# A two-layer streaming encoder step on one core: small attention and GLA products issued as closed clusters of one array shape

## The chip, the core and the metric

The kernel runs on one core of a Trainium2 chip. The metric is the device time of one execution in microseconds (us); before the change it is 2438.22 us, the median of three runs (2436.23 to 2441.65).

TensorE (PE) multiplies a stationary operand, which a weight load brings into its array of 128 by 128, with a moving operand, and writes to PSUM, which has eight banks of 128 partitions. A product whose stationary operand has fewer than 128 rows or columns uses a part of the array. The profile writes that shape as rows*columns (64*128). VectorE (DVE), ScalarE (ACT) and GpSimd (POOL) read the PSUM results and prepare operands. SyncE (SP) issues the DMAs.

## The reference, cut to what matters

Two layers; 2048 prompt tokens and 8 samples of 16 tokens, which are handled as 17 tiles of 128 tokens (the last one is the samples).

```
u = rms_norm(h) @ w_in                       # 1024 -> q, k, v, gate a, q b, k b, v b, gate b, forget gate
A = softmax(q k^T / 8, with a sink) v        # 8 heads of 64, 2 k/v heads, window of 128, in chunks of 64
B = gated linear attention (GLA), 4 heads, keys 64, values 128:
    S[t] = exp(g[t]) * S[t-1] + k[t] v[t]^T,   o[t] = q[t] S[t]
h = h + [A * silu(ga) ; rms_norm(B) * silu(gb)] @ w_out
h = h + sigmoid(rms_norm(h) @ w_pg) * (p @ w_pe)
```

For a prompt tile GLA is computed from products of 128 tokens: scores of the tile's own tokens with one another (masked; exponents are taken relative to a position near the pair, so the scores come from several scaled copies of queries and keys), scores times values, queries times the state S from the tiles before, and the update of S. Each of the eight samples has a state of its own, and for attention a cache of 128 older keys and values.

## The kernel before

The token tiles form five groups (0-2, 3-6, 7-10, 11-13, 14-16; the samples are tile 16). For each of two layers and five groups `phase_in` runs the projections and both attentions, then `phase_out` runs w_out, w_pg and w_pe. All weights are streamed from memory in pieces of 256 KB, which SP fetches and ACT (line 154) and DVE (line 84) split in a high and a low part. A big product is done in three passes, high by high, high by low, low by high (`mm3`, lines 322 to 324), each with a full 128*128 stationary operand and 256 to 512 moving columns.

Everything small is in plain fp32, whose products show as two records each. For a prompt tile, in the function and with the lines that the profile names:

- `attn_prompt`: scores L526, four products for each of two head pairs, 64*128, into two banks of the tag "s"; `softmax` (the exponentials are L487); the transposes L537, L538, L540 of the probabilities P; ACT and DVE copies to `ptf` and `pth`; outputs L560 (128*64) and L569 (64*64), eight products into two banks of the tag "o"; then `gate_mix` on DVE.
- `gla_exps` and `gla_scores`: E holds six scaled copies of queries and keys. Scores come from L733 (64*128), L738 (64*32) and L742 (64*64), 16 products in two banks "s"; a masked copy on DVE; L756 transposes the keys for the state update.
- `gla_prompt`: at·v L795 (128*128), E·S L798 (64*128), both into two banks "o"; the state update L802 (128*64).
- `gla_norm_gate` squares the output on ACT (L765), scales on POOL (L766, L768) and multiplies on DVE (L771); `gla_out` transposes it (L782) and writes the operand `mix` of w_out on ACT (L784) and DVE (L785).

For the sample tile `attn_sample` alternates a product with the cache (L623) and one with the new values (L624). `gla_sample` goes sample by sample: it loads a state by DMA, multiplies it with the queries (L834, transposed result), updates it (L840), and at the end copies the transposed results (line 856) and adds them to the output by products with the identity (L860), between the products L859.

The attention and GLA of each tile are Python generators that are put in a background queue, up to two at a time; `pump` advances them between the big products of the projections behind which they are to lie. This fixes priorities only. The scheduler orders each engine's instructions by priority and by when operands become ready, so a small cluster can be cut by big products or by another generator's rows.

PSUM before: two banks "mm" for big products, two "s", two "t", two "o". Where attention does not run, big products rotate through "mm", "s" and "o" (`pw`).

## Time and profile before

| what | value |
|---|---|
| median of three runs | 2438.22 us |
| span of the profiled execution, first to last instruction | 2437.0 us |
| instructions | 44522 |
| POOL's share, and that of the DMA queue of the weights | 28%, 36.7% of 16 engines |
| big products, passes of 256 columns into "mm" (six groups of 544 records) | about 157 us busy each |
| mean granted TensorE clock | 0.992 |

The profile is one execution taken apart by engine. A group of instructions is a line of the program, an engine, an operation and its tiles; "busy" is its time, the mean is that of one instruction. Since matmuls are pipelined, a mean is longer than the distance from one start to the next, so what a product costs in the stream is read from starts in the timeline. "xN" is the number of records. Releasers (after "<-") say what ended a wait.

### The profile page before, as it was taken

The numbers are of one execution on the slowest core, as the hardware profiler recorded it, in microseconds if no ns is written. First come the engines' busy times: TensorE is split into PE (matmuls) and PEld (weight loads), VectorE is DVE, ScalarE is ACT, GpSimd is POOL, SyncE is SP. The second block draws the span as 40 slices with busy tenths as digits, with TensorE's granted clock in tenths as the row PEclk, the third lists the DMA queues.
The fourth block names the chain that finished last, engine by engine and source line by source line (L and its number), as shares of the span: only waits on it lengthen the run. The fifth ranks groups of instructions, "written<-read, shape, count | busy, mean of one in ns | idle before, by whom it ended". The sixth has DMA issues, their size and how long they took to land.

```text
span 2437.0 us, 44522 instructions
## 1 busy us (share of the span) xinstructions
PE 2402.9 (99%) x16188; PEld 2151.0 (88%) x16188; DVE 1661.0 (68%) x3957; ACT 1304.1 (54%) x3087; POOL 691.0 (28%) x833
## 2 busy tenths in 40 slices
PE   8999999999999999999999999999999999999999
PEld 8899888897888989988998998888988889899889
DVE  7767765777567867764876687567775588577645
ACT  6556644555445655643665566445554456466434
POOL 4224212341214312422332152123312143133222
PEclk9999999999999999999999999999999999999999
DMA  5245222432144325523532442134321543355233
GB/s 161 87 137 153 83 70 92 139 116 80 36 150 147 103 79 176 160 85 108 170 114 87 158 144 85 55 116 137 105 71 35 168 144 101 100 163 153 86 103 123
DMA packets 160443, 279.15 MB, mean 115 GB/s; under 512 B 17840, under 2 KB 43824, under 8 KB 160224
## 3 DMA queue, kind: packets, MB, share of 16 engines
q1 hardware_dynamic: 159536, 275.43, 36.7%
q8 instruction: 127, 2.08, 0.4%
q10 hardware_dynamic: 688, 0.88, 0.1%
q14 instruction: 92, 0.75, 0.1%
HBM read 255.41 MB, written 20.71 MB: 113 GB/s over the span
## 4 chain that ended last, share of the span: by engine, by line
PE 90%; DVE 4%; DMA 2%; ACT 2%; issue 2%; POOL 0%; SPq 0%; DVEq 0%; POOLq 0%; ACTq 0%
PE pw L324 13%; PE pw L322 13%; PE pw L323 13%; PE mm L322 11%; PE mm L323 11%; PE mm L324 11%; PE s L526 3%; DVE w L84 2%; PE o L560 1%; PE s L733 1%; PE o L795 1%; DMA raw<-in_w_pe_dram 1%; PE o L798 1%; PE o L569 1%; PE t L802 1%
## 5 line engine op out<-in xcount | busy, mean ns | idle before, releaser
L84 DVE TENSOR_TENSOR w<-raw,w 128x512 fp32r<-128x512 f32 (+1 forms) x800 | 565.9, 748 | 60.3 <-ACT w L154 58.2
L154 ACT ACTIVATE w<-raw 128x512 fp32r<-128x512 f32 (+1 forms) x800 | 452.0, 625 | 138.6 <-DMA raw<-in_w_pe_dram 34.1
L324 PE MATMUL pw<-mix,w 128*128 128x384 f32 (+1 forms) x640 | 228.2, 360 | 0.0
L322 PE MATMUL pw<-mix,w 128*128 128x384 f32 (+1 forms) x640 | 226.6, 362 | 1.6 <-ACT mix L784 1.6
L323 PE MATMUL pw<-mix,w 128*128 128x384 f32 (+1 forms) x640 | 228.0, 358 | 0.0
L84 POOL TENSOR_TENSOR ot<-gth,hst 128x384 f32<-128x384 f32 (+1 forms) x79 | 103.1, 1306 | 249.3 <-DVE gth L1017 208.0
L487 ACT ACTIVATE P<-s,nm 128x192 f32<-128x192 f32 (+3 forms) x272 | 108.7, 413 | 108.8 <-DVE den L480 90.6
L322 PE MATMUL mm<-w,A 128*128 128x256 f32 x544 | 159.9, 294 | 0.0
L322 PE MATMUL mm<-w,B 128*128 128x256 f32 x544 | 159.9, 294 | 0.0
L323 PE MATMUL mm<-w,B 128*128 128x256 f32 x544 | 157.2, 289 | 0.0
L323 PE MATMUL mm<-w,A 128*128 128x256 f32 x544 | 156.9, 288 | 0.0
L324 PE MATMUL mm<-w,B 128*128 128x256 f32 x544 | 156.2, 287 | 0.0
L324 PE MATMUL mm<-w,A 128*128 128x256 f32 x544 | 156.1, 287 | 0.0
L84 POOL TENSOR_TENSOR acc<-sq,acc 128x384 f32<-128x384 f32 (+1 forms) x60 | 75.3, 1254 | 252.3 <-ACT sq L253 251.8
L84 POOL TENSOR_TENSOR E<-E,qkb 128x128 f32<-128x128 f32 (+1 forms) x160 | 105.0, 687 | 122.2 <-DVE qkb L670 48.7
L322 PEld LDWEIGHTS pw<-mix,w 128*128 128x128 f32 x640 | 120.4, 189 | 13.5 <-ACT mix L784 2.0
L324 PEld LDWEIGHTS pw<-mix,w 128*128 128x128 f32 x640 | 120.7, 189 | 10.9 <-issue 0.6
L84 POOL TENSOR_TENSOR xacc<-sq,xacc 128x384 f32<-128x384 f32 (+1 forms) x66 | 98.2, 1488 | 111.4 <-ACT sq L253 109.4
L323 PEld LDWEIGHTS pw<-mix,w 128*128 128x128 f32 x640 | 120.7, 189 | 10.0
L84 POOL TENSOR_TENSOR mix<-ga_t,mix 128x512 fp32r<-128x512 f32 x34 | 43.8, 1287 | 288.1 <-ACT mix L507 288.1
L322 PE MATMUL mm<-B,w 128*128 128x384 f32 (+1 forms) x320 | 117.8, 368 | 1.9 <-DVE yq L377 1.9
L322 PE MATMUL mm<-A,w 128*128 128x384 f32 (+1 forms) x320 | 117.3, 366 | 0.7 <-DVE yq L377 0.7
(279 smaller groups left out, 7327.4 us busy)
## 6 DMA issues: line engine op xcount, KB each, us to landing
raw<-in_w_in_dram SPq DMA_DIRECT2D x400, 256.0 KB, 3.3
raw<-in_w_out_dram SPq DMA_DIRECT2D x160, 256.0 KB, 3.3
raw<-in_w_pg_dram SPq DMA_DIRECT2D x160, 256.0 KB, 3.8
raw<-in_w_in_dram SPq DMA_DIRECT2D x40, 272.0 KB, 3.3
raw<-in_w_pe_dram SPq DMA_DIRECT2D x40, 256.0 KB, 3.6
hl<-in_h_dram SPq DMA_DIRECT2D x24, 192.0 KB, 3.5
hbuf<-ot SPq DMA_DIRECT2D x24, 192.0 KB, 2.8
hx<-hbuf SPq DMA_DIRECT2D x24, 192.0 KB, 4.0
```

What stands on the lines that cost most here:

```text
L84: (eng or G).tensor_tensor(out=out, in0=in0, in1=in1, op=op1)
L154: A.activation(out=w[:, 0, k0:k0 + 2, :], in_=r, func=ACTF.Copy)
L322: PE.matmul(out=out, lhsT=sh, rhs=mh, start=(i == 0), stop=False)
L323: PE.matmul(out=out, lhsT=sh, rhs=ml, start=False, stop=False)
L324: lastmm[0] = PE.matmul(out=out, lhsT=sl, rhs=mh, start=False, stop=(i == last)).ins
L487: A.activation(out=P[:, e, p0:p0 + wd], in_=ps[:, c, :wd], func=ACTF.Exp, scale=0.125, bias=nm[:, e:e + 1], accum_out=den[:, 0, e:e + 1])
L526: PE.matmul(out=lst[g][:, c, :wd], lhsT=qT[gs, ti, c * 256 + hp * 128:c * 256 + hp * 128 + 128], rhs=kk[gs, k0:k0 + wd], start=True, stop= ...
L560: PE.matmul(out=ot[c][gs], lhsT=vT[:, fs, gs], rhs=ptf[:, c, g], start=True, stop=not half)
L569: PE.matmul(out=ot[c][gs], lhsT=vT[hr, hf, gs], rhs=pth[hr, g], start=not full, stop=True)
L733: PE.matmul(out=pa[e][:, hp, :], lhsT=E[hs, 1, hp, :], rhs=E[hs, 0, hp, :], start=True, stop=True)
L795: PE.matmul(out=po[h % 2][:, hp, :], lhsT=at[:, h, :], rhs=vt[:, h * 128:h * 128 + 128], start=True, stop=False)
L798: PE.matmul(out=po[h % 2][:, hp, :], lhsT=E[hs, 5, hp, :], rhs=S[hs, hp, :], start=False, stop=True)
```

## The change

The products of a cluster are issued through a new function `chain`: the first one carries, as additional dependences, the last operands that the later ones need, and each later one is ordered behind its predecessor at high priority, so that nothing comes between. The two-bank tiles "s" and "o" replace pairs of one-bank tiles, and are held in a pool of their own (`banks_as("p")`) while attention runs; otherwise the four banks are single tiles for big products (`banks_as("w")`), and `pw` takes every third tile from "mm".

In `softmax` and in the masked copy of the GLA scores one instruction covers both banks where there were two. The GLA scores are cut in pieces of 64 rows by 32 columns (32 products in place of 16 for a prompt tile; the quarter that L733 computed only for L742 to overwrite is left out). In `gla_prompt` the four products of each kind follow one another. In `attn_sample` the 16 products with the cache come first, then the 16 with the new values. In `gla_sample` the states come in by two DMAs; the queries are spread over a masked copy `Em` (POOL), and queries times state go straight into the output accumulation, without the transposed intermediate, its copy and the identity products. Comments and doc strings are removed, which moves lines: `mm3` is L343 to L345, the attention transposes are L556, L557, L559, the key transposes L789, the output transposes L815.

```diff
-    ps_s = ctx.enter_context(tc.tile_pool(name="ps_s", bufs=2, space=bass.MemoryType.PSUM))
     ps_t = ctx.enter_context(tc.tile_pool(name="ps_t", bufs=2, space=bass.MemoryType.PSUM))
-    ps_o = ctx.enter_context(tc.tile_pool(name="ps_o", bufs=2, space=bass.MemoryType.PSUM))
+    banks = dict(pool=None, stack=None, n=0)
+
+    def banks_as(kind):
+
+        if banks["stack"] is not None:
+            banks["stack"].close()
+            banks["stack"] = None
+        if kind is None:
+            return
+        banks["n"] += 1
+        banks["stack"] = ExitStack()
+        banks["pool"] = banks["stack"].enter_context(
+            tc.tile_pool(name=f"ps_{kind}{banks['n']}", bufs=1, space=bass.MemoryType.PSUM, reuse_waits="tile"))
...
-        """any bank, where attention does not run"""
         rot[0] += 1
-        p, tg = ((ps_m, "mm"), (ps_s, "s"), (ps_m, "mm"), (ps_o, "o"), (ps_s, "s"), (ps_o, "o"))[rot[0] % 6]
-        return p.tile([128, n], F32, tag=tg, name="pw")
-
-    def po2(shape):
-        return [ps_o.tile(shape, F32, tag="o", name="o") for _ in range(2)]
-
-    def ps2(shape):
-        return [ps_s.tile(shape, F32, tag="s", name="s") for _ in range(2)]
+        if rot[0] % 3 == 1:
+            return pm(n)
+        return banks["pool"].tile([128, 512], F32, tag="w", name="pw", bufs=4)[:, :n]
+    def pair(tag):
+        return banks["pool"].tile([128, 2, 512], F32, tag=tag, name=tag, bufs=1)
+    def chain(prev, after=(), **kw):
+        if prev[0] is None:
+            prev[0] = PE.matmul(**kw).ins
+            for x in after:
+                tc.add_manual_dep(prev[0], x.name, mybir.DependencyInfo(mybir.DependencyClass.Sync, mybir.DependencyReason.DATA),
+                                  reason="operands of the products behind it")
+        else:
+            with tc.issue_after(prev[0]), tc.high_priority():
+                prev[0] = PE.matmul(**kw).ins
 
...
-                lst = [ps_s.tile([128, 2, 192], F32, tag="s", name="s") for g in range(2)]
+                lst = pair("s")[:, :, :384].rearrange("p g (c k) -> p g c k", c=2)
+                pv = [None]
...
-                        PE.matmul(out=lst[g][:, c, :wd], lhsT=qT[gs, ti, c * 256 + hp * 128:c * 256 + hp * 128 + 128],
-                                  rhs=kk[gs, k0:k0 + wd], start=True, stop=True)
+                        chain(pv, out=lst[:, g, c, :wd], lhsT=qT[gs, ti, c * 256 + hp * 128:c * 256 + hp * 128 + 128],
+                              rhs=kk[gs, k0:k0 + wd], start=True, stop=True)
...
-            ot = po2([128, 256])
+            ot = pair("o")[:, :, :256]
+            pv = [None]
...
-                        PE.matmul(out=ot[c][gs], lhsT=vT[:, fs, gs], rhs=ptf[:, c, g], start=True, stop=not half)
+                        chain(pv, (pr_, pq_), out=ot[gs, c], lhsT=vT[:, ti + c, gs], rhs=ptf[:, c, g], start=True, stop=not half)
...
+            ot = pair("o")[:, :, :256]
+            pv = [None]
+            for b in range(8):
+                for g in range(2):
+                    gs = slice(g * 64, g * 64 + 64)
+                    bc = slice((b % 4) * 64, (b % 4) * 64 + 64)
+                    chain(pv, out=ot[gs, b // 4, bc], lhsT=cv[:, b, gs], rhs=pts[g][0][:, b * 64:b * 64 + 64],
+                          start=b % 4 == 0, stop=False, skip_group_check=True)
+            for b in range(8):
+                for g in range(2):
+                    gs = slice(g * 64, g * 64 + 64)
+                    bc = slice((b % 4) * 64, (b % 4) * 64 + 64)
+                    chain(pv, out=ot[gs, b // 4, bc], lhsT=vo[b // 4][:, b % 4, gs], rhs=pts[g][1][:, b * 64:b * 64 + 64],
+                          start=False, stop=True, skip_group_check=True)
...
+                Em = ip.tile([128, 2, 2, 128], F32, name="Em")
+                G.memset(Em, 0.0)
...
+                for par in range(2):
+                    G.tensor_copy(Em[:, par].rearrange("p h (c two i) -> p two h c i", two=2, i=16)[:, par],
+                                  E[:, 0].rearrange("p h (c two i) -> p two h c i", two=2, i=16)[:, par])
...
-            ptt(E[:, 3, :, 64:128], E[:, 3, :, 64:128], qv[:, :, 64:128], ALU.mult)
+            done["e3"] = G.tensor_tensor(out=E[:, 3, :, 64:128], in0=E[:, 3, :, 64:128], in1=qv[:, :, 64:128], op=ALU.mult).ins
...
-            pa = ps2([128, 2, 128])
+            if sample:
+                E = E[0]
+            pa = pair("s")[:, :, :256].rearrange("p e (h t) -> p e h t", h=2)
             both = [slice(0, 64), slice(64, 128)]
+            pv = [None]
             for hp in range(2):
-                for e, hs in enumerate(both):
-                    PE.matmul(out=pa[e][:, hp, :], lhsT=E[hs, 1, hp, :], rhs=E[hs, 0, hp, :], start=True, stop=True)
+                for i in range(4):
+                    q = slice(32 * i, 32 * i + 32)
+                    k = slice(0, 64 if i < 2 and not sample else 128)
+                    for e, hs in enumerate(both):
+                        chain(pv, (done["e3"],), out=pa[q, e, hp, k], lhsT=E[hs, 1, hp, q], rhs=E[hs, 0, hp, k], start=True, stop=True)
                 if sample:
                     continue
                 for i in range(2):
                     for e, hs in enumerate(both):
-                        PE.matmul(out=pa[e][64 * i:64 * i + 32, hp, 64 * i + 32:64 * i + 64],
-                                  lhsT=E[hs, 2, hp, 64 * i:64 * i + 32], rhs=E[hs, 2, hp, 64 * i + 32:64 * i + 64],
-                                  start=True, stop=True)
-                for e, hs in enumerate(both):
-                    PE.matmul(out=pa[e][0:64, hp, 64:128], lhsT=E[hs, 3, hp, 0:64], rhs=E[hs, 3, hp, 64:128],
+                        chain(pv, out=pa[64 * i:64 * i + 32, e, hp, 64 * i + 32:64 * i + 64],
+                              lhsT=E[hs, 2, hp, 64 * i:64 * i + 32], rhs=E[hs, 2, hp, 64 * i + 32:64 * i + 64],
+                              start=True, stop=True)
+                for i in range(2):
+                    q = slice(32 * i, 32 * i + 32)
+                    for e, hs in enumerate(both):
+                        chain(pv, out=pa[q, e, hp, 64:128], lhsT=E[hs, 3, hp, q], rhs=E[hs, 3, hp, 64:128],
                               start=True, stop=True)
...
-            po = po2([128, 2, 128])
-            for hp in range(2):
-                for h in (2 * hp, 2 * hp + 1):
-                    PE.matmul(out=po[h % 2][:, hp, :], lhsT=at[:, h, :], rhs=vt[:, h * 128:h * 128 + 128], start=True, stop=False)
-                for h in (2 * hp, 2 * hp + 1):
-                    hs = slice((h % 2) * 64, (h % 2) * 64 + 64)
-                    PE.matmul(out=po[h % 2][:, hp, :], lhsT=E[hs, 5, hp, :], rhs=S[hs, hp, :], start=False, stop=True)
+            po = pair("o")[:, :, :256].rearrange("p e (h t) -> p e h t", h=2)
+            pv = [None]
+            for h in range(4):
+                chain(pv, deps, out=po[:, h % 2, h // 2, :], lhsT=at[:, h, :], rhs=vt[:, h * 128:h * 128 + 128], start=h < 2, stop=False,
+                      skip_group_check=True)
+            for h in range(4):
+                hs = slice((h % 2) * 64, (h % 2) * 64 + 64)
+                chain(pv, out=po[:, h % 2, h // 2, :], lhsT=E[hs, 5, h // 2, :], rhs=S[hs, h // 2, :], start=False, stop=True,
+                      skip_group_check=True)
             pu = pt([128, 2, 128])
             for h in range(4):
                 hp, hs = h // 2, slice((h % 2) * 64, (h % 2) * 64 + 64)
-                PE.matmul(out=pu[hs, hp, :], lhsT=ke[:, h * 64:h * 64 + 64], rhs=vt[:, h * 128:h * 128 + 128],
-                          start=True, stop=True)
+                chain(pv, out=pu[hs, hp, :], lhsT=ke[:, h * 64:h * 64 + 64], rhs=vt[:, h * 128:h * 128 + 128],
+                      start=True, stop=True)
...
+            st8 = []
+            for c in range(2):
+                x = ip.tile([128, 4, 2, 128], F32, tag="ptf", name="s0", bufs=2)
+                SP.dma_start(out=x, in_=a["s0"][l, 4 * c:4 * c + 4].rearrange("b p h v -> p b h v"))
+                st8 += [x[:, b] for b in range(4)]
+            yield
+            pv = [None]
+            for c in range(4):
+                pu = pt([128, 2, 2, 128])
+                for b in range(2):
+                    km = ip.tile([128, 256], F32, tag="qy", name="km", bufs=4)
+                    G.tensor_scalar(out=km, in0=ke, scalar1=cst[:, C_OH + 2 * c + b:C_OH + 2 * c + b + 1], scalar2=None, op0=ALU.mult)
+                    for h in range(4):
+                        hp, hs = h // 2, slice((h % 2) * 64, (h % 2) * 64 + 64)
+                        chain(pv, out=pu[hs, b, hp, :], lhsT=km[:, h * 64:h * 64 + 64], rhs=vt[:, h * 128:h * 128 + 128],
+                              start=True, stop=True)
...
+                yield
+            while sgb[ti] is None:
+                yield
+            po = pair("o")[:, :, :256].rearrange("p e (h t) -> p e h t", h=2)
+            for h in range(4):
+                chain(pv, out=po[:, h % 2, h // 2, :], lhsT=at[:, h, :], rhs=vt[:, h * 128:h * 128 + 128], start=h < 2, stop=False,
+                      skip_group_check=True)
             for b in range(8):
+                tb = slice(b // 2 * 32, b // 2 * 32 + 32)
                 for h in range(4):
+                    hs = slice((h % 2) * 64, (h % 2) * 64 + 64)
+                    chain(pv, out=po[tb, h % 2, h // 2, :], lhsT=Em[hs, b % 2, h // 2, tb], rhs=st8[b][hs, h // 2, :],
+                          start=False, stop=b % 2 == 1, skip_group_check=True)
```

What this does to the order on PE, at three places of layer 0. In each row stand the line, the operation, output and inputs, the output's size, and how many alike follow one another.

First, the GLA output of one prompt tile and the GLA scores of the next, in the second group (`at` the masked scores, `vb` the values, `S` the state, `ke` the scaled keys, `E` scaled queries and keys). PE before:

```order
L795 MATMUL o<-vb,at_89 128x128 x2
L798 MATMUL o<-S,E 128x128 x2
L795 MATMUL o<-vb,at_89 128x128 x2
L798 MATMUL o<-S,E 128x128 x2
L802 MATMUL t<-vb,ke 64x128 x4
L733 MATMUL s<-E 128x128 x2
L738 MATMUL s<-E 32x32 x4
L742 MATMUL s<-E 64x64 x2
L733 MATMUL s<-E 128x128 x2
L738 MATMUL s<-E 32x32 x4
L742 MATMUL s<-E 64x64 x2
L756 MATMUL t<-cst,E 128x128 x2
```

PE of the changed kernel at the same place (L116 is the first product of a chain, L122 the later ones):

```order
L116 MATMUL o<-vb,at_83 128x128
L122 MATMUL o<-vb,at_83 128x128 x3
L122 MATMUL o<-S,E 128x128 x4
L122 MATMUL t<-vb,ke 64x128 x4
L116 MATMUL s<-E 32x64
L122 MATMUL s<-E 32x64 x3
L122 MATMUL s<-E 32x128 x4
L122 MATMUL s<-E 32x32 x4
L122 MATMUL s<-E 32x64 x8
L122 MATMUL s<-E 32x128 x4
L122 MATMUL s<-E 32x32 x4
L122 MATMUL s<-E 32x64 x4
```

The output's three kinds now stand once each, and the scores, all of one stationary shape, have no change of it within the cluster.

Second, attention in the second group (`kT`, `qs` keys and queries, `P` probabilities, `ptf`, `pth` their transposes, `vT` values). PE before:

```order
L526 MATMUL s<-kT,qs 128x192 x2
L560 MATMUL o<-ptf,vT 64x256 x4
L569 MATMUL o<-pth,vT 64x256 x3
L537 MATMUL t<-cst,P 128x128
L569 MATMUL o<-pth,vT 64x256
L538 MATMUL t<-cst,P 128x128
L540 MATMUL t<-cst,P 128x128
L537 MATMUL t<-cst,P 128x128
L538 MATMUL t<-cst,P 128x128
L540 MATMUL t<-cst,P 128x128
L526 MATMUL s<-kT,qs 128x192 x2
```

PE of the changed kernel, the nearest clusters of the same group:

```order
L116 MATMUL s<-kT,qs 128x192
L122 MATMUL s<-kT,qs 128x192 x3
L556 MATMUL t<-cst,P 128x128
L557 MATMUL t<-cst,P 128x128
L559 MATMUL t<-cst,P 128x128
L556 MATMUL t<-cst,P 128x128
L557 MATMUL t<-cst,P 128x128
L559 MATMUL t<-cst,P 128x128
L345 MATMUL mm<-w,B_2334 128x256
```

The four score products stand together, where each half of two stood by itself before, with outputs and transposes of another tile between.

Third, the end of the group with the samples (`km`, `ats` the sample's masked keys and scores, `s_...` its states, `on` the normed output, `mix_...` operands of w_out). PE before:

```order
L802 MATMUL t<-vb,ke 64x128 x4
L834 MATMUL s<-Es,s_12942 128x16 x4
L322 MATMUL pw<-mix_11168,w 128x384
L323 MATMUL pw<-mix_11168,w 128x384
L324 MATMUL pw<-mix_11168,w 128x384
L840 MATMUL t<-vb,km 64x128 x4
L859 MATMUL o<-vb,ats 128x128 x2
L860 MATMUL o<-cst,ga_t 128x128
L859 MATMUL o<-vb,ats 128x128
L860 MATMUL o<-cst,ga_t 128x128
```

PE of the changed kernel:

```order
L345 MATMUL mm<-mix_11307,w 128x384
L122 MATMUL t<-vb,km 64x128 x8
L122 MATMUL t<-vb,ke 64x128 x4
L122 MATMUL o<-vb,ats 128x128 x4
L122 MATMUL o<-s_12891,Em 32x128 x16
L122 MATMUL o<-s_12893,Em 32x128 x16
L815 MATMUL t<-cst,on 128x128 x8
L343 MATMUL pw<-mix_11307,w 128x384
```

The update, the output and the state products follow one another without big products between them, and the transposes of the normed output of two tiles (`on`, x8) come directly behind.

More of the change, by code (lines that the diff above doesn't have):

```diff
@@ L479, in softmax @@
[L479 to L488 removed]
+            mv = mx.rearrange("p (i c) -> p i c", c=2)
@@ L489, in softmax @@
+            for e in range(4):
+                wd = ps.shape[3] if wd_of is None else wd_of[e % 2]
+                p0 = 0 if wd_of is None else 128 - 64 * (e % 2)
+                A.activation(out=P[:, e, p0:p0 + wd], in_=ps[:, e // 2, e % 2, :wd], func=ACTF.Exp, scale=0.125,
+                             bias=nm[:, e:e + 1], accum_out=den[:, 0, e:e + 1])
             A.activation(out=den[:, 1], in_=den[:, 1], func=ACTF.Exp)
@@ L568, in attn_prompt @@
                     if half:
-                        PE.matmul(out=ot[c][gs], lhsT=vT[hr, hf, gs], rhs=pth[hr, g], start=not full, stop=True)
+                        chain(pv, out=ot[gs, c], lhsT=vT[hr, ti + 1 - c, gs], rhs=pth[hr, g], start=not full, stop=True)
             gate_mix(ot, ti, 2)
@@ L751, in gla_scores @@
             av = at.rearrange("p (hp e) t -> p e hp t", e=2)
-            for e in range(2):
-                V.copy_predicated(av[:, e], m.unsqueeze(1).to_broadcast([128, 2, 128]), pa[e])
+            V.copy_predicated(av, m.unsqueeze(1).unsqueeze(1).to_broadcast([128, 2, 2, 128]), pa)
             pk = pt([128, 256])
@@ L1075, in hybrid_step @@
     S = None
+    banks_as("w")
     for i, (l, gi) in enumerate(seq):
```

133 lines of the change are left out of this document (44 added, 89 removed).

## The prediction, as it was made before the changed kernel had run

> **What bounds the kernel now.** I read the page's busy times first, then the chain of work that ended last, then the waits of PE.
>
> ```profile
> PE 2402.9 (99%) x16188; PEld 2151.0 (88%) x16188; DVE 1661.0 (68%) x3957; ACT 1304.1 (54%) x3087; POOL 691.0 (28%) x833
> PE 90%; DVE 4%; DMA 2%; ACT 2%; issue 2%; POOL 0%; SPq 0%; DVEq 0%; POOLq 0%; ACTq 0%
> PE pw L403 <- ACT w L154: 7.2, 1, 7.2
> PE pw L322 <- ACT gth L1014: 5.4, 2, 2.7
> PE mm L322 <- DVE yq L377: 2.7, 2, 1.9
> ```
>
> TensorE is busy 99% of the span and makes up 90% of the chain. The longest single wait of PE (7.2 us) is for weights. In the whole list of waits one small product of attention or GLA stands: L834, with 2.7 us (its row is below). The operands of the others are ready when PE comes to them. So a microsecond taken out of PE's own stream is a microsecond of the span, as long as no operand becomes late. The question is what the small products cost in that stream, and that is read from the timeline of PE: start, duration, and how many records a group has (one fp32 product is two records).
>
> ```profile
> 390.69 0.60 PE L795 MATMUL o<-vb,at 128*128 128x128 f32 x4
> 391.23 0.49 PE L798 MATMUL o<-S,E 64*128 64x128 f32 x4
> 391.65 0.71 PE L795 MATMUL o<-vb,at 128*128 128x128 f32 x4
> 392.29 0.49 PE L798 MATMUL o<-S,E 64*128 64x128 f32 x4
> 392.71 0.66 PE L802 MATMUL t<-vb,ke 128*64 128x128 f32 x8
> 393.30 0.49 PE L733 MATMUL s<-E 64*128 64x128 f32 x4
> 393.72 0.27 PE L738 MATMUL s<-E 64*32 64x32 f32 x8
> 393.92 0.33 PE L742 MATMUL s<-E 64*64 64x64 f32 x4
> 394.18 0.49 PE L733 MATMUL s<-E 64*128 64x128 f32 x4
> 394.60 0.27 PE L738 MATMUL s<-E 64*32 64x32 f32 x8
> 394.79 0.33 PE L742 MATMUL s<-E 64*64 64x64 f32 x4
> 395.06 0.44 PE L756 MATMUL t<-cst,E 128*128 128x128 f32 x2
> ...
> 395.45 0.28 PE L323 MATMUL mm<-w,B 128*128 128x256 f32 x1
> 395.57 0.28 PE L324 MATMUL mm<-w,B 128*128 128x256 f32 x1
> L795 PE MATMUL o<-vb,at 128*128 128x128 f32 x256 | 43.5, 289 | 0.0
> L738 PE MATMUL s<-E 64*32 64x32 f32 x512 | 17.7, 203 | 0.0
> ```
>
> This is the GLA output of one prompt tile (2.61 us, 390.69 to 393.30) and the GLA scores of the next (1.76 us, 393.30 to 395.06). The stationary shapes (128*128, 64*128, 128*64, 64*32, 64*64) change at each row. Two readings:
>
> - **The rate inside a shape.** Four records of L795 take 0.60 us where one takes 0.289 on average: (0.60 - 0.289) / 3 = 0.104 us a record, 0.81 ns a column.
> - **The price of a change of shape.** L733 has two products on two row halves, so two records of 128 columns one after the other: 2 x 0.104 = 0.21 of the 0.42 us until the next group starts; 0.21 is left over. L742: 0.26 - 2 x 64 x 0.81 ns = 0.16. L738: 0.20 - 2 x 32 x 0.81 ns = 0.15. I take 0.18 us a change.
>
> L738 also shows that pieces lying in different parts of the array run together: eight records end 0.27 us after the first began, and one takes 0.203, so they start (0.27 - 0.203) / 7 = 10 ns apart.
>
> **The change part by part.**
>
> *GLA scores.* 16 products in three shapes become 32 in one (64 rows by 32 columns), over two row halves and four column quarters. The busiest of the eight places (the first column quarter) gets, for each pair of heads, 64 + 32 + 64 columns, so 320 columns, in two records each: 640 x 0.81 ns = 0.52 us; with one change, 0.70; I take 0.75 for places that wait on one another. Against 1.76: 1.0 x 32 prompt tiles = **32 us**. Before, these clusters are also broken up by the scheduler, 51 visits for the 32 tiles; 19 fewer visits at two changes each (0.36) are **7 us**. Bounds: if only the two row halves ran at once, each half has 64 + 64 + 128 + 128 + 32 + 32 + 64 + 64 = 576 columns for each of two pairs of heads, so 2 x 576 x 2 x 0.81 ns + 0.18 = 2.05 us with the weight loads hidden. With a load of 32 columns (26 ns at the same rate) shown at each of a half's 32 records it is 2.9 us. That would lose 9 to 36 us. With no entry cost it is 0.52, a gain of 40.
>
> [...]
>
> *GLA output.* Instead of 2, 2, 2, 2, 4 products, 4, 4, 4. Eight records of at·v are 8 x 0.104 + 0.18 = 1.01 (before 0.54 + 0.64 = 1.18), four products E·S on two halves 4 x 0.104 + 0.18 = 0.60 (before 0.84), ke·v stays at 0.59. 2.61 becomes 2.20: 0.41 x 32 = **13 us**.
>
> *Attention scores.* The scheduler splits many clusters of four products in two visits: 97 visits for 64 clusters.
>
> ```profile
> 92.37 0.28 PE L324 MATMUL mm<-w,A 128*128 128x256 f32 x1
> 92.58 0.92 PE L526 MATMUL s<-kT,qs 64*128 64x192 f32 x4
> 93.42 0.39 PE L322 MATMUL mm<-w,A 128*128 128x256 f32 x1
> 93.64 0.28 PE L323 MATMUL mm<-w,A 128*128 128x256 f32 x1
> ...
> 286.87 0.39 PE L323 MATMUL mm<-B,w 128*128 128x512 f32 x1
> 287.10 0.39 PE L324 MATMUL mm<-B,w 128*128 128x512 f32 x1
> 287.42 0.93 PE L526 MATMUL s<-kT,qs 64*128 64x192 f32 x8
> 288.27 0.50 PE L322 MATMUL mm<-B,w 128*128 128x512 f32 x1
> 288.61 0.40 PE L323 MATMUL mm<-B,w 128*128 128x512 f32 x1
> ```
>
> A big product of 256 columns has a slot of 0.12 us (395.45 to 395.57), one of 512 columns 0.23 (286.87 to 287.10). Half a cluster (four records) costs 93.64 - 92.37 - 2 x 0.12 = 1.03 us, a whole one (eight) 288.61 - 287.10 - 2 x 0.23 = 1.05. Half costs as much as all, because its two products sit on the same row half and follow one another, where the whole fills both halves. A split that goes saves 1.03 where both halves stood alone, and about two changes, 0.36, where one half stood beside other small work. I take 0.7 x 33 visits = **23 us**.
>
> *Attention output.* The same products, 49 visits to 32: 17 x 0.36 = **6 us** (two changes each).
>
> *Big products after a visit.* The first one takes 93.64 - 93.42 = 0.22 instead of 0.12. Of the visits above, and those of the sample below, some 90 go: **9 us**.
>
> *Sample tile, once a layer.*
>
> ```profile
> 1073.12 0.33 PE L623 MATMUL o<-ptf,cv 128*64 128x64 f32 x2
> 1073.38 0.32 PE L624 MATMUL o<-pto,vo 16*64 16x64 f32 x2
> ...
> 1060.00:1074.00 14.00, 14.00 (x118) 11.40 (x116) 11.01 (x32) 9.43 (x30) 5.88 (x7) 1.00 0.26 77
> 1074.60:1084.80 10.20, 10.20 (x51) 8.25 (x50) 4.31 (x11) 1.96 (x5) 2.35 (x3) 0.50 0.00 0
> 1136.00:1139.40 3.40, 3.40 (x19) 2.63 (x17) 1.69 (x6) 0.00 (x0) 0.93 (x1) 0.50 0.27 93
> 2289.70:2296.50 6.80, 6.80 (x34) 5.86 (x35) 4.35 (x12) 1.75 (x4) 2.36 (x3) 0.50 0.00 0
> 2347.70:2351.10 3.40, 3.40 (x20) 2.51 (x16) 1.35 (x5) 0.00 (x0) 0.93 (x1) 0.51 0.24 80
> L834 PE MATMUL s<-Es,s 64*128 64x16 f32 x128 | 10.0, 262 | 2.7 <-DMA s<-in_s_dram 2.7
> ```
>
> The 32 output products of a layer alternate between two shapes, one every 0.26 us: 8.3 us. In two clusters, on two column halves, each is 8 x 2 records x 64 columns x 0.81 ns + 0.18 = 1.0, so 2.0 in all: 6 x 2 layers = **12 us**. The state products L834 (busy 10.0 us in both layers) and the identity products behind them go, for 32 a layer in the one shape of 64*32, four at each of eight places: 4 x 2 x 0.104 + 0.18 = 1.0 us. I count 10.0 - 2 x 1.0 = **8 us**.
>
> In these rows of the table of windows the third number from the end is PE's granted clock (1.00 in the first row, 0.50 in the others). At half clock PE loses half of the window. The windows at 1074 and 2289 lie on this alternating output and what follows it, those at 1136 and 2347 on the sample's GLA: 10.2 + 6.8 + 3.4 + 3.4 = 23.8 us, so **12 us** are lost, and I let them go with the alternation. [...] The 2.7 us that L834 waits for its state go too, as the state is loaded earlier: **3 us**.
>
> *Transposes and other small rows.* Fewer visits: **4 us**. DVE loses one reduction and one masked copy a cluster, which stand beside PE's work: nothing.
>
> Saved: 32 + 7 + 13 + 23 + 6 + 9 + 12 + 8 + 12 + 3 + 4 = **129 us**.
>
> *New waits.* A closed cluster needs all of its operands at its head, and what stands behind it on PE's queue waits with it. Three places where the order of PE leaves too little work in front:
>
> ```profile
> 1123.53 0.28 ACT L765 ACTIVATE gsq<-o 128x128 f32<-128x128 f32 x1 [0.71 <-PE o L798]
> 1126.70 1.13 DVE L771 SCALAR_TENSOR_TENSOR on<-o,gss,sgb 128x128 f32<-128x128 f32 x4 [1.87 <-POOL gss L768]
> ```
>
> - At the end of the sample's group the transposes of its output stand right behind its product cluster. The way from those products through ACT, POOL and DVE to the transposes took 1126.70 + 1.13 - 1123.53 = 4.3 us, and nothing covers it; with the start of the transposes 5 us, and perhaps 2 more at half clock afterwards: 7 x 2 layers = 14.
> - Five bursts of transposes at the ends of query blocks have no big product between them; the nearest row is L322 on yq above, 2.7 us for two: 5 x 1.35 = 7.
> - Attention output clusters that follow each other within a microsecond, at four places, an estimated 0.85 us each (the second waits until DVE has read the two banks that the first filled): 3.
>
> Together **24 us**; the bounds are 0 (the operands are early) and 50 (each twice as long).
>
> The sum is made against the span of the profiled execution (2437.0): 2437.0 - 129 + 24 = 2332. The median of the runs is 1.2 us above the span. I forecast **2332**.
>
> **The rivals.**
>
> 1. *The pieces run side by side on the row halves only.* Then a tile's scores take 2.05 to 2.9 us in place of 0.75: 42 to 69 us more, 2374 to 2401. For it: no row of before has eight places at once, and L526 pairs only row halves. Against it: L738's four places on two halves. [...]
> 2. *Slower: the heads of closed clusters wait.* There are about 170 of them (five for each of 32 prompt tiles, some five for each sample tile). If the last operand of each (the pth copy on DVE, the E products on POOL) comes late, PE stands still with its queue. The point from which it decides is (129 - 24) / 170 = 0.62 us a cluster; at 1 us each the kernel takes 2332 + 170 = 2502. For it: one late operand now holds four to 32 products. Against it: PE waits nowhere for such operands now, and big products stand between most of the clusters.
> 3. *The gain is taken by DVE or ACT.* DVE is busy 79% of an attention stretch (11.01 of 14 us at 1060), and its work stays nearly what it was. If the 129 us saved turned into waits on it for two fifths, the time would be 2332 + 50 = 2382.
> 4. *The half clock stays* where the sample's products are short, for another reason than the alternation: 2332 + 12 = 2344. [...]
> 5. *The order does not change as the words say.* This I exclude: in the order of PE, changes of shape (transposes counted as 128*128) go from 864 to 414. At 0.18 each these 450 alone are 81 us; with the halves that again run side by side (23) and the lost clock (12) that is near the sum.
>
> **How the numbers follow.** The forecast 0.65 (2292 to 2360), rival 4 0.12 (inside that range), rival 1 0.08, rival 3 0.07, rival 2 0.06, no difference 0.02. The range is to hold 8 in 10: below stands the sum with the new waits at nearly nothing and more of the splits at their full 1.03, 2292; above the sum with the waits at 50 and a part of rival 3, or the near end of rival 1, 2384. It leaves out rival 2, most of rival 1 and part of rival 3. A run of this kernel can tell about 0.2% (5 us) from no change. Faster 0.92, same 0.02, slower 0.06.
>
> **What would show it.** Right: the groups of the score pieces take about 0.75 us a tile in the timeline; L526's successors stand in groups of eight records of 0.6 to 0.9 us; no half clock at the sample's output; PE's wait list has the transposes of the sample's output with some 5 us. Wrong: score clusters of 2 us or more (rival 1); the half clock at the sample's output as before (rival 4); PE busy below 96% with waits at the heads of clusters (rivals 2 and 3). The forecast fails most easily in the new waits, which no row of before shows.

## The result and the profile after

| | median | runs | ratio to before, 95% interval |
|---|---|---|---|
| before | 2437.98 us | 2436.23 to 2441.65 | |
| changed | 2375.86 us | 2373.43 to 2377.86 | 0.9745 [0.9731, 0.9759] |

The kernel before has a fourth run here, so its median is 2437.98 us. The changed kernel is 62 us faster. The forecast was 105 us faster, so 43 us are missing. First the page of the changed kernel: busy times and instructions of each engine, then the chain of work that ended last by engine.

```profile
PE 2300.5 (97%) x17244; PEld 2094.9 (88%) x17244; DVE 1637.6 (69%) x3851; ACT 1302.4 (55%) x3083; POOL 683.5 (29%) x839
PE 79%; DVE 7%; ACT 6%; issue 3%; DMA 3%; POOL 2%; DVEq 0%; SPq 0%; POOLq 0%; ACTq 0%
```

PE is busy 102.4 us less, but stands idle 2374.5 - 2300.5 = 74.0 us of its span, where it was 34.1 before (2437.0 - 2402.9). TensorE's share of the chain falls from 90 to 79%: work of DVE, ACT and POOL now ends waits that nothing covers. The list of PE's waits names them (line waited at, releaser: total us, times, longest):

```profile
PE t L815 <- DVE on L804: 26.3, 9, 3.9
PE pw L343 <- ACT w L175: 9.5, 5, 2.6
PE mm L424 <- ACT w L175: 7.9, 1, 7.9
PE pw L345 <- DVE w L95: 3.9, 4, 1.3
PE t L441 <- DVE abT L444: 3.1, 2, 2.2
PE o L116 <- DVE ga_t L524: 2.7, 4, 0.7
```

The first row is new: the transposes of the normed GLA output (L782 before) wait nine times, for 26.3 us. Two of the nine stand at the groups with the samples, with 3.7 us each; the other seven, 18.9 us, stand at the ends of prompt groups. The second row, products of w_pe that wait for weights split by ACT, is new too. The third is the wait for the first weights, which was there before with 7.2.

What the clusters themselves cost is read from PE's timeline: the GLA output of one prompt tile, and the GLA scores of the next.

```profile
380.90 0.38 PE L116 MATMUL o<-vb,at 128*128 128x128 f32 x2
381.12 0.83 PE L122 MATMUL o<-vb,at 128*128 128x128 f32 x6
381.88 0.71 PE L122 MATMUL o<-S,E 64*128 64x128 f32 x8
382.53 0.66 PE L122 MATMUL t<-vb,ke 128*64 128x128 f32 x8
383.11 0.24 PE L116 MATMUL s<-E 64*32 64x64 f32 x1
383.12 0.33 PE L122 MATMUL s<-E 64*32 64x64 f32 x7
383.19 0.22 PE L116 MATMUL s<-E 64*32 64x64 f32 x1
383.20 0.84 PE L122 MATMUL s<-E 64*32 64x64 f32 x55
383.97 0.44 PE L789 MATMUL t<-cst,E 128*128 128x128 f32 x2
```

The output takes 383.11 - 380.90 = 2.21 us, and 64 records of score pieces take 383.97 - 383.11 = 0.86 us, 13 ns a record. So the pieces do run side by side, and on more places than the two row halves, for which the estimate was 2.05 us.

Then the end of the first group, all engines. Before (PE's rows of w_out products between are left out):

```profile
143.99 0.66 PE L802 MATMUL t<-vb,ke 128*64 128x128 f32 x8
144.17 0.28 ACT L765 ACTIVATE gsq<-o 128x128 f32<-128x128 f32 x1
...
146.32 0.35 POOL L766 TENSOR_SCALAR gss<-gss,cols 128x4 f32<-128x4 f32 x1 [10.03 <-ACT gsq L765]
...
147.80 1.13 DVE L771 SCALAR_TENSOR_TENSOR on<-o,gss,sgb 128x128 f32<-128x128 f32 x4 [1.59 <-POOL gss L768]
...
150.95 0.49 PE L782 MATMUL t<-cst,on 128*128 128x128 f32 x3
```

And the changed kernel at the same place, with its last product ahead of the transposes:

```profile
141.19 0.66 PE L122 MATMUL t<-vb,ke 128*64 128x128 f32 x8
142.22 1.28 ACT L175 ACTIVATE w<-raw 128x512 fp32r<-128x512 f32 x2 [1.30 <-DMA raw<-in_w_out_dram]
...
143.41 0.26 ACT L798 ACTIVATE gsq<-o 128x128 f32<-128x128 f32 x1
143.47 0.34 PE L345 MATMUL mm<-mix,w 128*128 128x384 f32 x1
...
145.07 0.35 POOL L799 TENSOR_SCALAR gss<-gss,cols 128x4 f32<-128x4 f32 x1 [10.65 <-ACT gsq L798]
...
146.54 1.13 DVE L804 SCALAR_TENSOR_TENSOR on<-o,gss,sgb 128x128 f32<-128x128 f32 x4 [1.84 <-POOL gss L801]
147.04 1.01 PE L815 MATMUL t<-cst,on 128*128 128x128 f32 x4 [3.23 <-DVE on L804]
```

From the start of the state update (`t<-vb,ke`) through ACT, POOL and DVE to the start of `on` it takes 147.80 - 143.99 = 3.81 us before and 146.54 - 141.19 = 5.35 in the changed kernel, where ACT first waits 1.30 us for a weight of w_out and splits it, and only then starts the norm (`gsq`). The larger difference is in what covers this way. Before, big products of w_out that need the attention half of `mix` alone stood in front of the transposes until 150.95; now they end at 143.47 and PE waits 3.23 us. In PE's order the number of big products between a group's last prompt cluster and these transposes was 36 to 41 at the eight prompt groups; it is 10, 12, 24, 10, 22, 12, 12, 22 in the changed kernel, and all of them are in the two mm banks (`mm<-mix`). The fewer there are, the longer PE waits: behind 24 it does not wait, behind 22 it waits 1.9 and 2.6 us, behind 12 it waits 2.2 to 2.8, and behind 10 it waits 3.2 and 3.9.

The table of windows behind that wait (busy us of PE, PEld, DVE, ACT, POOL; PE's granted clock, the DMA share and GB/s last):

```profile
142.00:147.04 5.04, 1.80 (x11) 1.51 (x10) 2.31 (x6) 2.62 (x10) 1.35 (x2) 1.00 0.71 212
147.04:148.20 1.16, 1.16 (x6) 0.86 (x7) 0.63 (x3) 0.11 (x1) 0.00 (x0) 0.98 0.90 299
148.20:151.60 3.40, 3.40 (x13) 3.40 (x12) 1.71 (x2) 1.42 (x2) 0.00 (x0) 0.50 0.99 326
151.60:160.00 8.40, 8.40 (x50) 8.40 (x49) 2.57 (x5) 2.53 (x5) 0.00 (x0) 1.00 0.25 91
```

After the wait PE runs 3.4 us at a clock of 0.50, so the wait costs another 1.7.

### The profile page after: what moved, and what is told of

It reads as the page before. It is cut to its first block, busy times and chain, and to the rows that moved or that the text cites. A ratio compares the mean times of both kernels' runs of the same rounds, so it can differ in the third digit from the quotient of the medians.

```text
span 2374.5 us, 46429 instructions
## 1 busy us (share of the span) xinstructions
PE 2300.5 (97%) x17244; PEld 2094.9 (88%) x17244; DVE 1637.6 (69%) x3851; ACT 1302.4 (55%) x3083; POOL 683.5 (29%) x839
## 4 chain that ended last, share of the span: by engine, by line
PE 79%; DVE 7%; ACT 6%; issue 3%; DMA 3%; POOL 2%; DVEq 0%; SPq 0%; POOLq 0%; ACTq 0%
PE mm L343 14%; PE mm L345 14%; PE mm L344 13%; PE pw L343 9%; PE pw L345 9%; PE pw L344 8%; PE o L122 3%; DVE w L95 3%; PE s L122 2%; PE s L116 1%; DMA raw<-in_w_out_dram 1%; PE o L116 1%; PE t L122 1%; ACT w L175 1%; PE t L556 1%
## 5 line engine op out<-in xcount | busy, mean ns | idle before, releaser
L343 PE MATMUL mm<-w,B 128*128 128x256 f32 (+1 forms) x688 | 200.2, 291 | 0.0
L344 PE MATMUL mm<-w,B 128*128 128x256 f32 (+1 forms) x688 | 196.3, 285 | 0.0
L345 PE MATMUL mm<-w,B 128*128 128x256 f32 (+1 forms) x688 | 196.1, 285 | 0.0
L343 PE MATMUL mm<-w,A 128*128 128x256 f32 (+1 forms) x664 | 193.3, 291 | 0.0
L344 PE MATMUL mm<-w,A 128*128 128x256 f32 (+1 forms) x664 | 189.8, 286 | 0.0
L345 PE MATMUL mm<-w,A 128*128 128x256 f32 (+1 forms) x664 | 189.4, 285 | 0.0
L343 PE MATMUL pw<-mix,w 128*128 128x384 f32 (+1 forms) x424 | 156.1, 370 | 0.0
L343 PE MATMUL mm<-B,w 128*128 128x384 f32 (+1 forms) x424 | 154.1, 363 | 1.1 <-DVE zm L975 1.0
L344 PE MATMUL pw<-mix,w 128*128 128x384 f32 (+1 forms) x424 | 155.1, 367 | 0.0
L345 PE MATMUL pw<-mix,w 128*128 128x384 f32 (+1 forms) x424 | 154.8, 367 | 0.0
L343 PE MATMUL mm<-A,w 128*128 128x384 f32 (+1 forms) x424 | 153.6, 362 | 0.0
L344 PE MATMUL mm<-A,w 128*128 128x384 f32 (+1 forms) x424 | 153.2, 361 | 0.0
L345 PE MATMUL mm<-A,w 128*128 128x384 f32 (+1 forms) x424 | 152.8, 360 | 0.0
L345 PE MATMUL mm<-B,w 128*128 128x384 f32 (+1 forms) x424 | 152.7, 360 | 0.0
L344 PE MATMUL mm<-B,w 128*128 128x384 f32 (+1 forms) x424 | 152.3, 359 | 0.0
L343 PEld LDWEIGHTS mm<-w,B 128*128 128x128 f32 x688 | 131.4, 191 | 5.9 <-issue 4.2
L345 PEld LDWEIGHTS mm<-w,B 128*128 128x128 f32 x688 | 131.3, 191 | 1.4 <-issue 1.3
```

Source lines behind the costliest of these rows:

```text
L343: PE.matmul(out=out, lhsT=sh, rhs=mh, start=(i == 0), stop=False)
L344: PE.matmul(out=out, lhsT=sh, rhs=ml, start=False, stop=False)
L345: lastmm[0] = PE.matmul(out=out, lhsT=sl, rhs=mh, start=False, stop=(i == last)).ins
```

## The experiments

All edits are to the changed kernel. Times are medians, to be held against its 2375.9; the kernel before, measured beside each set, had 2436.8 to 2439.0. Spans and waits are of the profiled runs.

| run | edit | median | against changed |
|---|---|---|---|
| e1_rot | counter of the bank rotation set to zero | 2351.9 | -24.0 |
| e2_banks | two permanent pools, big products in halves of the pairs | 2538.6 | +162.7 |
| e3_open | clusters not closed | 2406.0 | +30.2 |
| e4_scores3 | GLA scores in three shapes | 2393.5 | +17.6 |
| e5_twopools | a pool for s, one for o, counter set to zero | 2325.9 | -49.9 |
| e6_samplefirst | e5, sample's output before its updates | 2327.9 | -47.9 |
| e7_oldsample | sample path of before | 2400.3 | +24.4 |
| e8_alternate | GLA output in shapes 2, 2, 2, 2, 4 | 2384.7 | +8.9 |
| e9_pools_only | e5 without setting the counter | 2351.2 | -24.7 |
| e10_two_scores3 | e5 with e4's scores | 2353.7 | -22.2 |

### Where the missing time is: e1, e2, e5, e9

My theory was that the banks are at fault: `phase_out` opens its pool over four banks that the pair tiles `s` and `o` hold, so its products wait until `o` is read by the norm, while `s` has long been free. Before, mm and s were open to w_out. The rival was that ACT, busy with weights, makes the norm late.

e1 adds one line:

```diff
         banks["n"] += 1
+        rot[0] = 0
```

> The changed kernel, with one line more: the counter that picks the banks of the big products is set to zero where phase_out opens its pool, so that the first and the fourth unit of w_out, and no longer only one of the first three, are in an mm bank. In the order of PE 22 to 24 big products then stand between the last GLA cluster of every prompt group and the transposes of its output, where the changed kernel has 10 to 12 at five of eight places. Theory (the banks that the two-bank tiles hold take away the cover of these transposes): the list of PE's waits has L815 on DVE with 26.3 us in 9 places now, and it falls to 12 to 17; with a half-clock window or two less the time is 2355 to 2366, against 2375.9. Rival (the transposes wait because ACT and POOL are late with the norm, whatever PE has in front): L815 keeps over 23 us and the time stays within 5 us of 2375.9.

Measured 2351.9, ratio to before 0.965 [0.963, 0.9669]. The wait on `on` is 13.5 us in 7 places, as expected, and the clock is 0.995 in place of 0.991:

```profile
PE t L816 <- DVE on L805: 13.5, 7, 3.7
...
PE pw L346 <- DVE w L96: 6.5, 5, 1.3
...
PE pw L344 <- ACT w L176: 1.4, 2, 0.7
```

The time fell by 3 us more than expected. The waits of w_pe products on ACT's weights (the second row of the changed kernel's list), which the expectation did not have, fell from 9.5 to 1.4 us, while those on DVE's weights rose from 3.9 to 6.5.

e2 was meant to free `s` early and failed:

```diff
+    ps_s = ctx.enter_context(tc.tile_pool(name="ps_s", bufs=1, space=bass.MemoryType.PSUM))
+    ps_o = ctx.enter_context(tc.tile_pool(name="ps_o", bufs=1, space=bass.MemoryType.PSUM))
...
+        if half[0] is None:
+            half[0] = pair("s" if rot[0] % 6 < 3 else "o")
+            return half[0][:, 0, :n]
+        x, half[0] = half[0], None
+        return x[:, 1, :n]
```

> The changed kernel, with its closed clusters and two-bank tiles, but the tiles s and o in two pools that stay open all the time, and big products outside attention taking halves of them; the counter set to zero at the head of phase_out as in the run beside it. Then s is free for w_out while o is still read: 34 to 36 big products stand before the transposes at the eight ends of prompt groups (before the change 36 to 41), none or three at the two sample groups as in the changed kernel. Theory (lost cover by the banks): the wait of L815's successor falls from 26.3 to some 8 us (the two sample groups), half-clock windows after those waits go, 2340 to 2355. Rival (ACT and POOL late): within 5 us of 2375.9. Second rival (whole pairs as the unit of waiting for big products cost what the cover brings): 2365 to 2376.

Measured 2538.6, slower than before (1.0416 [1.0399, 1.0434]). Its list of waits:

```profile
PE mm L342 <- DVE gth L1045: 36.3, 10, 4.9
PE o L342 <- DVE yq L397: 33.3, 10, 3.8
PE s L342 <- DVE ab L435: 20.1, 5, 4.4
...
PE t L814 <- DVE on L803: 6.3, 2, 3.1
```

The last row did what was expected (two sample groups left). But big products outside attention now wait for DVE: PE is idle 2537.8 - 2364.7 = 173.1 us, and at a clock of 0.967 another 84 us are lost. I read the second and third rows so, that a big product which wants a half of a pair waits until DVE has read both halves of the pair before it: my second rival, which I had put at no more than what the cover brings. The first row is on the mm banks, which are not halves of pairs, and was not followed. A remedy with a side effect of this size settles nothing, so e5 keeps single banks:

```diff
-        banks["pool"] = banks["stack"].enter_context(
-            tc.tile_pool(name=f"ps_{kind}{banks['n']}", bufs=1, space=bass.MemoryType.PSUM, reuse_waits="tile"))
+        rot[0] = 0
+        for x in "so":
+            banks[x] = banks["stack"].enter_context(
+                tc.tile_pool(name=f"ps_{kind}{x}{banks['n']}", bufs=1, space=bass.MemoryType.PSUM, reuse_waits="tile"))
...
-        return banks["pool"].tile([128, 512], F32, tag="w", name="pw", bufs=4)[:, :n]
+        return banks["s" if rot[0] % 6 in (2, 3) else "o"].tile([128, 512], F32, tag="w", name="pw", bufs=2)[:, :n]
```

> The changed kernel, but the tiles s and o each in a pool of their own, opened and closed together as the one pool was, two one-bank tiles for big products in each outside attention, and the counter of the rotation set to zero when they open, so that w_out's units go to mm, s, s, mm and only then to the banks of o. In PE's order 36 to 39 big products stand between the last GLA cluster of each of the eight prompt groups and the transposes of its output (before the change 36 to 41, changed kernel 10 to 24, counter alone 22 to 24), and at the two sample groups 15. Theory (one pool over four banks makes w_out wait for the last reader of o, which takes the cover of these transposes): the wait on L804's successor falls to 6 us or less, half-clock windows to five or fewer, 2332 to 2347. Rival (a second cause, as ACT's weight splitting, sets the ends once the counter is set): 2348 to 2356, as the counter alone gave.

Measured 2325.9, 0.9539 [0.9524, 0.9553]: 50 us less than the changed kernel, by nothing but which bank the big products get and when it is open. That is 6 us below what the theory gave. The span is 2323.2 us, PE idle 42.4. The wait that had 26.3 us, and the longest others of this run:

```profile
PE mm L426 <- ACT w L177: 7.8, 2, 7.6
PE pw L347 <- DVE w L97: 4.5, 5, 1.0
PE pw L345 <- DVE gth L1052: 4.2, 5, 1.0
...
PE t L817 <- DVE on L806: 2.1, 2, 1.1
```

The granted clock, from the table of cores, of the changed kernel:

```profile
core 0: 2374.5 us, clock 0.991
```

and of e5:

```profile
core 0: 2323.2 us, clock 0.998
```

Before it was 0.992. The share that the clock takes, (1 - clock) x span, is 19.5 us before, 21.4 in the changed kernel and 4.6 in e5. These three are sure to about 1 us, as the clock is given to three digits. With the waits at the group ends (26.3 us in the changed kernel, 2.1 in e5) most of what the half clock cost goes as well, 16.8 of 21.4 us.

The rival, ACT late with the norm, has a share in how long the way to `on` is, but not in whether PE waits. At the four groups of three prompt tiles the time from the end of the last output product to the start of `on` is 3.7 to 4.0 us before, 5.3 to 6.8 in the changed kernel and 4.8 to 6.1 in e5. So e5 has ACT nearly as late, and waits at none of them.

e9 has the two pools, and not the line `rot[0] = 0`.

> The kernel with the two pools, without setting the counter to zero. In PE's order 22 to 39 big products stand before the transposes of the eight prompt groups' ends (counter alone 22 to 24, both 36 to 39), none or three at the sample groups. Theory (what counts is the cover, however it is had): between the counter alone (2351.9) and both (2325.9), with waits of 8 to 12 us on the output transposes: 2332 to 2345. Rival (the two pools are the whole gain, or the counter is): within 3 us of 2325.9, or of 2351.9.

Measured 2351.2 (0.9652 [0.9634, 0.967]), outside what the theory gave and equal to the counter alone. The rival's time was met, but not its reading that one edit is the whole gain, as both together give 25 us more. Its waits say why:

```profile
PE t L816 <- DVE on L805: 10.2, 5, 3.7
PE pw L344 <- ACT w L176: 9.5, 6, 3.2
```

The cover returned in part (10.2 us left), but the waits for ACT's weights stay, which the counter removes. So the two edits do different things: the pools give cover, the counter gives cover and takes most of these 9.5 us away. How the counter does the latter was not followed further.

### What the parts of the change are worth: e3, e4, e10, e8, e7

e3 replaces `chain` by a plain product. Its accumulations start product by product, and terms of some heads are lost from the GLA and sample outputs; the products are the same in number and size.

```diff
-        if prev[0] is None:
...
-            with tc.issue_after(prev[0]), tc.high_priority():
-                prev[0] = PE.matmul(**kw).ins
+        PE.matmul(**kw)
```

> The changed kernel with chain issuing plain products: no order behind the predecessor, no high priority, no wait of the first product for the later ones' operands. Pieces of 64x32, two-bank tiles and the sample's new path stay. In PE's order the changes of shape go from 414 to 542, and the cover of the group ends stays as it is (10 to 24 products). Theory (a change of shape costs 0.18 us, and a split score cluster runs one row half at a time): 128 x 0.18 = 23 us, and some 10 us for halves and first big products: 2400 to 2415. Rival (the heads of closed clusters wait, and what closing saves it gives back): within 6 us of 2375.9, or below.

Measured 2406.0 (0.9872 [0.9857, 0.9887]): closing the clusters is worth 30 us, as the theory had it.

```profile
PE 2330.3 (97%) x17244; PEld 2106.3 (88%) x17244; DVE 1642.4 (68%) x3851; ACT 1301.4 (54%) x3083; POOL 685.2 (29%) x839
```

PE is busy 29.8 us more. The clock is 0.989, so 26.4 us of it are the clock's share, 5 more than in the changed kernel; the other 25 are 0.19 us for each of the 128 changes of shape with the slow first products behind. The heads of closed clusters do not give it back. e3 is not the order of before: in PE's order the scores of attention stand in 73 visits, where the changed kernel has 64 and before there were 97.

e4 issues the scores in the three shapes of before, within a chain.

```diff
-                for i in range(4):
-                    q = slice(32 * i, 32 * i + 32)
...
+                for e, hs in enumerate(both):
+                    chain(pv, (done["e3"],), out=pa[:, e, hp, :], lhsT=E[hs, 1, hp, :], rhs=E[hs, 0, hp, :], start=True, stop=True)
```

> The changed kernel with the GLA scores in the 16 products and three shapes of before, still in a closed chain and in the two-bank tile. 160 changes of shape more (574). Theory (shape changes and side-by-side pieces as read from the timeline: 0.86 us a tile for the pieces, 1.76 for the three shapes): 32 x 0.9 = 29 us more, 2398 to 2410. Rival (the pieces save on PE what another engine then waits for): less than 15 us more.

Measured 2393.5 (0.9817 [0.9798, 0.9836]), 17.6 more, between theory and rival. The page has PE busy 23.3 us more at a clock of 0.993, so without the clock's share (16.7 us, where it was 21.4) 28.0 more:

```profile
PE 2323.8 (97%) x16172; PEld 2105.8 (88%) x16172; DVE 1636.5 (68%) x3851; ACT 1300.8 (54%) x3083; POOL 682.9 (29%) x839
```

and the list of waits has for the transposes

```profile
PE t L810 <- DVE on L799: 20.3, 9, 3.7
```

That left open whether the pieces are worth 17.6 or 29 us. e10 repeats the edit where the ends hardly wait.

> The kernel with two pools and the counter, with the GLA scores in 16 products and three shapes as in the run on the changed kernel, where that cost 17.6 us in place of 29, while PE's busy time rose by 23 and waits and half clock at the ends fell. Here the ends hardly wait. Theory (the pieces are worth 0.9 us a tile, and at the ends of the changed kernel a part of it was given back): 26 to 31 us more than 2325.9, 2352 to 2357. Rival (the pieces are worth 17 to 18 us wherever they stand): 2342 to 2345.

Measured 2353.7, 27.7 more than e5: as the theory had it. The pieces are worth 28 us, and on the changed kernel e4 gave 10 of them back: the wait on `on` is 6.0 us less there and the clock's share 4.7.

e8 lets the GLA output alternate, at v, E S, at v, E S:

```diff
-            for h in range(4):
-                chain(pv, deps, out=po[:, h % 2, h // 2, :], lhsT=at[:, h, :], rhs=vt[:, h * 128:h * 128 + 128], start=h < 2, stop=False,
-                      skip_group_check=True)
...
+            for hp in range(2):
+                for h in (2 * hp, 2 * hp + 1):
+                    chain(pv, deps, out=po[:, h % 2, hp, :], lhsT=at[:, h, :], rhs=vt[:, h * 128:h * 128 + 128], start=True, stop=False)
+                for h in (2 * hp, 2 * hp + 1):
...
+                    chain(pv, out=po[:, h % 2, hp, :], lhsT=E[hs, 5, hp, :], rhs=S[hs, hp, :], start=False, stop=True)
```

> The changed kernel with the products of gla_prompt in the order of before, two of at v, two of E S, two of at v, two of E S, still in one closed chain: 64 changes of shape more (478), the same products, the same clusters. Theory (0.18 us a change): 11.5 us more on PE, 2383 to 2391. Rival (what a change costs is hidden by the loads of the next weights): within 4 us of 2375.9.

Measured 2384.7 (0.9782 [0.9768, 0.9797]). The theory holds. PE is busy 2313.8 us at the same clock, 13.3 more for 64 changes: 0.21 us each. The time rose by 8.9; the waits at the ends fell by 2.1 us.

e7 puts the sample's path of before back.

```diff
-                    chain(pv, out=po[tb, h % 2, h // 2, :], lhsT=Em[hs, b % 2, h // 2, tb], rhs=st8[b][hs, h // 2, :],
+                    PE.matmul(out=pT[:, h % 2, hp, bc], lhsT=x[hs, hp, :], rhs=E[hs, 0, hp, bc], start=True, stop=True)
...
+                chain(pv, out=po[:, h % 2, hp, :], lhsT=oT[:, h, :], rhs=ident, start=False, stop=True)
```

> The changed kernel with the sample's path of before: attention output alternating between cache and new values, states multiplied sample by sample into a transposed result, which ACT copies and identity products add. Everything for the prompt stays. Theory as the prediction had it (12 us of alternation, 8 us of state products, 3 us of waiting for states, 12 us of half clock at these places, less some 8 us of waits at the sample groups' ends that go): 2395 to 2405. Rival (half-clock windows belong to waits of PE, not to the alternation): no window at the sample's attention output, 2384 to 2394.

Measured 2400.3 (0.9844 [0.9829, 0.9859]), as the theory had it. PE is busy 2329.7 us at a clock of 0.987, so without the clock's share (31.2 us) 19 more than in the changed kernel. Half-clock windows come back at the alternating output, which runs from 1052.0 to 1056.1 and from 1062.4 to 1066.5 us (and its twin in layer 1). The first row is the same place in the changed kernel, without one; the others are e7:

```profile
1050.00:1060.50 10.50, 10.50 (x132) 9.47 (x132) 7.59 (x23) 7.26 (x21) 3.56 (x3) 1.00 0.20 52
1056.70:1060.10 3.40, 3.40 (x18) 3.31 (x16) 1.93 (x7) 0.97 (x2) 0.00 (x0) 0.51 0.00 0
1066.90:1070.30 3.40, 3.40 (x18) 3.40 (x17) 3.19 (x13) 1.83 (x5) 0.80 (x2) 0.50 0.01 2
2247.90:2251.30 3.40, 3.40 (x17) 2.86 (x17) 0.61 (x2) 0.60 (x1) 0.00 (x0) 0.50 0.00 0
```

### The sample's end: e6

e6 takes e5 and issues the sample's output ahead of its updates, each in a chain of its own.

```diff
-            pv = [None]
             for c in range(4):
+                pv = [None]
                 pu = pt([128, 2, 2, 128])
```

> The kernel with two pools, and in gla_sample the output cluster (scores times values, states times queries) is issued ahead of the eight state updates and in a chain of its own; each pair of updates is a chain. The sample's output then stands some 48 big products ahead of its transposes. Theory (at the end of the sample groups PE waits for the norm of the sample's output, about 4 us a layer, with a half-clock window behind): 6 to 12 us less than the kernel with two pools. Rival (the updates, now last, hold the two t banks that the transposes need): within 3 us of it or slower.

Measured 2327.9, 2 us from e5: the rival. In e5 the 15 big products had left only 2.1 us at the two sample groups. In e6 those go, and PE waits there for the updates (`sn`, 2.9 us in all) and for `mix` (2.8 us) instead.

## Why the prediction was right or wrong

The direction, and the reason for it, were right; the size fell short by 43 us, most of it because of two steps. I split the difference of the spans (2374.5 against the sum's 2332) in three: PE's busy time without the clock's share, its idle time, and the clock's share.

- **PE's own stream was right in sum, and not shown in every part.** Busy time without the clock's share falls from 2402.9 - 19.5 = 2383.4 to 2300.5 - 21.4 = 2279.1, by 104 us; the sum without the clock (12) and the wait for states (3) was 114. The output of a tile is 2.21 us (forecast 2.20), the scores 0.86 (0.75, so 3.5 us of the 10 in 32 tiles), a change of shape 0.19 to 0.21 (0.18). Taken back one at a time, the parts cost this stream 25 us (closing, e3), 28 (the pieces, e4; forecast 32), 13 (the output, e8; 13) and 19 (the sample's path, e7; 20): 85 of 104. The other 19 are measured by no run; the 23 us that the sum had for the scores of attention, which e3 leaves mostly whole, may lie there.
- **"New waits" is the step that failed.** It put a wait at the transposes of the output only at the two sample groups, "two layers = 14". There it was near: 7.4 us, and 1.7 at half clock with each. The trace has seven more places, with 18.9 us, at the ends of prompt groups, and the 9.5 us of w_pe products on ACT's weights; the sum had neither. I counted what stands in front of the clusters and overlooked what w_out can put behind them: I read that the pair tiles take four banks, and did not follow when those banks come free for `phase_out`. PE's idle time rose by 39.9 us, against 17 (24 new, of which 4 were half clock, and 3 gone): 23 us.
- **The half clock, "12 us are lost, and I let them go", failed with it.** The windows at the sample went (e7 brings them back), but as many came with the new waits: seven of the nine have one, 13.7 us lost. The clock's share is 21.4 us in place of 19.5, against 12 less and 4 more: 10 us. Rival 4 had named this size, but for another cause. Of the four windows before, only those at 1074 and 2289 lay on the alternation; those at 1136 and 2347 began 1.4 and 1.5 us after waits of L834 for its state, and went with these.
- The rest, 43 - 23 - 10 = 10 us, is PE's stream.
- **Rival 1** (row halves only, 2.05 to 2.9 us) is out: a tile takes 0.86 us. Its upper end, with a load shown at each record, was the author's estimate, and no run shows it. **Rival 2** (heads of clusters): e3 shows the opposite, +30 without closing. **Rival 3**: DVE and ACT did come into the chain (7 and 6%), but not as load: DVE is busy 69% of the span, where it was 68.
- e5 comes to 2325.9, near the 2332 that were forecast, once the banks are open: the missing time was not in the idea of the change but in its pools and in the turn in which big products take the banks. That it comes so near is in part luck: against the sum, e5 has 9 us less of idle time and 7 less at half clock, and its stream takes 7 more.

## What to carry to other kernels

Where an array is filled by many small products, count the changes of shape in the order and price them from starts in the timeline (here 0.19 to 0.21 us each); close a cluster and let it keep one shape. When buffers are regrouped for that, ask at each phase boundary which later products they kept fed, and count in the order how much work stands in front of each long way over other engines; here that count could be taken from the order before any run. A wait is not over when its engine starts again: add the slow clock that can follow it (here with seven of nine, 13.7 us in all).

## What the runs showed of the hardware that was not expected

Half-clock windows of 3.4 us, once of 6.8, come in two ways here. One is with a wait of PE (147.04, then 0.50 from 148.20): of the nine waits at the transposes, seven, of 1.9 to 3.9 us, have a window that begins in their last 1.3 us or up to 1.7 us behind, and two, of 2.2 and 2.4 us, have none. The other is with PE shown busy all the time, after some 4 us of alternating, short products (e7, 3.40 of 3.40 us busy at 0.51 from 1056.7, where the alternation began at 1052.0); in two clusters the same products ran at 1.00 (changed kernel, 1050.0 to 1060.5). In the second the trace shows no idle time of PE, and why the clock falls there is not shown. And 64 records of 64*32 pieces ran at 13 ns a record.
